# Gate/up of the two feed-forward layers: the last two plain outputs go to other places, and the first combined unit is written in a fixed order on three engines

## The chip, the cores and the metric

One core of one Trainium2 chip runs the whole kernel. The metric is the device time of one execution in microseconds (us). TensorE (PE) does the matrix products, VectorE (DVE), ScalarE (ACT) and GpSimd (POOL) the elementwise work, and SyncE (SP) issues most transfers between memory and the on-chip store.

## The reference

One inference step of a two-layer decoder for a prompt of 1040 rows and 64 sample rows, which share all weights. The part that matters is the feed-forward step behind each layer:

```python
def swiglu(xn, w_gu, w_d):
    gu = xn @ w_gu
    return (jax.nn.silu(gu[..., :D_FF]) * gu[..., D_FF:]) @ w_d
```

`D_MODEL` is 1024 and `D_FF` 2816; the step is done twice, once per layer, as h = h + swiglu(rmsnorm(h)).

## The kernel before

**Tiling.** The 1104 rows lie along the free axis in three groups t = 0, 1, 2 of 336, 384 and 384 columns; a column block of 128 weights is stationary. Every float32 operand is split into a high part (rounded by ACT, `copy` or `Copy` with a scale) and a low part (source minus high part, on DVE), and each product is three matmuls: high by high, low by high, high by low. `self.split(src, hi, lo)` is one such pair of instructions for weights (lines L336 on ACT and L337 on DVE). For activations the pair is `m.cast(r, src)` (L145, or L147 with a sign) on ACT and `m.rest(r, src)` (L141, or L154 with a sign) on DVE.

**Gate and up** (`ffn`). The 22 blocks of 128 gate columns and 22 of up columns are worked as numbered pairs x: even x is gate, odd x is up, each of two blocks (f = 0, 1). Pairs 0 and 1 are "plain": `direct(x, t)` does 48 matmuls for one row group and returns two evictions, `ends`. For gate an eviction is ACT's Silu from the accumulator into a `spare` place. For up it is DVE's product of the accumulator with that place, and a transfer of the product to `hT` (lines L1484 and L1485):

```python
tt(out=o, in0=b, in1=o, op=ALU.mult)
nc.sync.dma_start(hT[t][:, f], o)
```

Pairs 2 to 21 are "combined" units. A `Unit(x)` uses 20 products of sums of weights with sums of activations instead of 24 (a fast matrix-multiplication scheme over 2 blocks x 3 row groups). `u.p(r, b)` is product r, six matmuls into bank b (L1331); `u.copy` moves a bank to a place c on ACT (L1337); `u.mark` adds or subtracts a bank and a place on DVE (L1306 adds, L1307 subtracts); `u.out` is ACT's Silu (L1353) for gate, or DVE's product with the kept gate value (L1350) and a transfer to `hT` for up. The places have names (s1, c15, s2, e, t4, v2); for unit 2 the rotation in `Unit.__init__` makes t4 the buffer `ns[:, 1]` and v2 the buffer `fs`, which are also the two `spare` places of row group 2.

`u.steps(v)` is a generator of four steps with 16 products, and the last four (19, 14, 6, 3) of a unit are done within the first two steps of the next (`v` is the unit before). In order: step 0 is 17, copy s1, 15, copy c15, 18, copy s2, 10. Step 1 is 8, copy e, mark e (which reads the bank of product 10), 9, copy t4, 2, copy v2, mark t4, 13. Product 13 is the first to write that bank anew, so it needs mark e done. Step 2 is 12, mark s1, 5, 16, mark s1, Silu, 1, mark v2, 4, mark v2, Silu. Step 3 is 7, mark t4, 11, mark c15, Silu, 0, mark c15, Silu.

**Weights of a unit.** `weights.load(x)` brings the two blocks of pair x with SP. `weights.sums(x, part)` makes 12 sums on POOL (L108) into staging places. `weights.split(x, g)` splits block g of the products' weights: blocks 0 to 4 are (17, 15, 18, 10), (8, 2, 9, 13), (12, 1, 5, 4), (14, 0, 11, 7) and (6, 3); products that lie side by side are one instruction (15, 18 and 10 are 768 columns wide, 17 alone 256).

**What sets the order.** The program is planned by a scheduler with a model of the engines' times. Under `manual_schedule` the named engines keep the written order. `order` pins PE, DVE and ACT from the last group of the projection before to the end of the plain pairs; then `order.close()`, and `with fixed()` pins PE alone for units 2 to 20. Instructions of ACT and DVE behind `order.close()` are placed where the scheduler's model has the engine free, also in front of pinned ones. Two more casts stand in the unit loop of unit 2: the activations of products 7 and 3 of row group 2 (`m.cast`, `m.rest`), in steps 1 and 2.

Of the kernel before, what the change touches and what calls it, by code (L numbers as in the profile page):

```python
# [11 lines left out]
ALU = mybir.AluOpType  # L12
# [18 lines left out]
SL = max(b - a for a, b in TS)  # L31
# [3 lines left out]
NF = DFF // P  # L35
# [90 lines left out]
class Mix:  # L126
# [7 lines left out]
    def y(self, k, t, n=SL):  # L134
        return self.H[t][:, 2 * k : 2 * k + 2, :n]
# [1144 lines left out]
def ffn(self, H, flat, l, weights, order, mix, small, each, after, end, early=None):  # L1280
# [3 lines left out]
    nc, I = self.nc, self.I  # L1284
# [4 lines left out]
    hT = [self.dram.tile([P, NF, n], F32, name=f"hT{l}_{t}") for t, n in enumerate(size)]  # L1289
    with self.pool(f"ffn{l}") as fp, self.pool(f"ffnp{l}", space=PSUM) as pp:  # L1290
# [7 lines left out]
        col = lambda h, o: flat[h][:, o : o + SL]  # L1298
# [6 lines left out]
        tt = nc.vector.tensor_tensor  # L1305
# [158 lines left out]
        m, y = mix, mix.y  # L1464
# [6 lines left out]
        def direct(x, t):  # L1471

            n, ends = size[t], []
            for f in range(2):
                w = [a.rearrange("p (k n) -> p k n", k=KT) for a in weights.plain(x, f)]
                b = bank("mp", "d")[:, :n]
                for j in range(KT):
                    k = 2 * (ks if t == 2 else (2, 1, 3, 0))[j // 2] + j % 2
                    a = [z[:, k % 2] for z in m.X[m.D[t][k // 2]]]
                    self.mm3(b, w[0][:, k], w[1][:, k], a[0], a[1], j == 0, j == KT - 1)  # L1480

                def evict(b=b, o=spare[t][f][:, :n], f=f):
                    if x:
                        tt(out=o, in0=b, in1=o, op=ALU.mult)  # L1484
                        nc.sync.dma_start(hT[t][:, f], o)  # L1485
                    else:
                        nc.scalar.activation(o, b, AF.Silu)
                ends.append(evict)
            return ends
# [73 lines left out]
        weights.split(2, 2)  # L1563
        ends[1]()
        weights.sums(3, slice(0, 9))
        order.close()
        with fixed():
            v = None
            for x in range(2, NF - 1):
                u = Unit(x)  # L1570
                for g, _ in enumerate(u.steps(v)):
                    if x == 2 and 0 < g < 3:
                        r, src = ((7, y(2, 2)), (3, y(3, 2)))[g - 1]
                        m.cast(r, src, -1.0)
                        m.rest(r, src, -1.0)
                    if g < 3:
                        if g < 1 or g < 2 < x:
                            weights.split(x, 3 + g)
                        weights.split(x + 1, g)
                    if g == 1:  # L1580
                        weights.sums(x + 1, slice(9, None))
                        if x + 2 < NF:
                            weights.load(x + 2)
                    if g == 3 and x + 2 < NF:
                        weights.sums(x + 2, slice(0, 9))
                v = u
        with fixed(E.DVE, E.Activation):
            u = Unit(NF - 1)
# [33 lines left out]
            for i, (t, z, c) in enumerate(seq):  # L1622
# [4 lines left out]
                for m in range(4):  # L1627
                    if lead:
                        acc[m] = bank("dps", "d")
                    o = acc[m][:, :n]  # L1630
# [19 lines left out]
                if i in (2, 16, 38):  # L1650
                    y = (2, 16, 38).index(i)
# [941 lines left out]
```

## Time and profile before

| what | value |
|---|---|
| median of 3 runs | 2955.42 us (2948.49 to 2958.77) |
| the profiled execution | 2959.27 us, span 2957.4 us |
| PE busy | 2836.6 us, 96% of the span |
| DVE, ACT, POOL busy | 1708.2, 1305.3, 999.5 us |
| units 2 to 21, first layer | from 635.9 us |
| units 2 to 21, second layer | from 2244.9 us |

A line of the timeline has the start in us, the length in us, the engine, the line of the kernel, the operation, what it writes and reads, its shape and a count; in brackets stands how long the engine had been idle before and what ended that. In the first layer the weights' raw places carry the name vA, in the second Ht; `slot`, `wl0` and `wl1` are weight places, `x0`, `x1`, `x2`, `T` and `U` activation places, `m` and `mp` accumulators. Matmuls overlap, so the distance of two starts tells more than a length.

### The profile page before, as it was taken

How to read it: one execution, taken by the hardware profiler on the slowest of the kernel's cores; microseconds unless marked ns; L12 is line 12 of the kernel's file. 1: busy time of each engine (PE TensorE's matmuls, PEld its weight loads, DVE VectorE, ACT ScalarE, POOL GpSimd, SP SyncE). 2: the span in 40 equal slices, each digit the busy share in tenths (PEclk: the TensorE clock that was granted, in tenths of full speed). 3: DMA queues.
4: the chain of work that ended last, by engine and by line, in shares of the span. 5: the costliest groups of instructions: out<-in, count | busy, mean ns of one | idle time of the engine just before them, and what ended most of it. 6: DMA issues, size and time to landing. Idle time of an engine off the chain costs nothing.

```text
span 2957.4 us, 53672 instructions
## 1 busy us (share of the span) xinstructions
PE 2836.6 (96%) x20542; PEld 2711.6 (92%) x20542; DVE 1708.2 (58%) x3406; ACT 1305.3 (44%) x2591; POOL 999.5 (34%) x1480
## 2 busy tenths in 40 slices
PE   7999997989999999999999899999998999999999
PEld 7998886989999999999999887777898999999998
DVE  5032456687777855463354442677467787765543
ACT  5122364344444444343344453777444444443432
POOL 2011223145556511104353101454315656541110
PEclk9999898999999999999999999999999999999999
DMA  7052446222222266544354676443412222227652
GB/s 224 7 134 86 117 112 186 82 62 76 79 77 85 84 244 214 172 152 152 125 166 136 200 286 216 152 157 101 143 55 72 80 81 78 78 83 262 211 183 102
DMA packets 300139, 392.79 MB, mean 133 GB/s; under 512 B 32238, under 2 KB 222698, under 8 KB 298858
## 3 DMA queue, kind: packets, MB, share of 16 engines
q1 hardware_dynamic: 262978, 270.05, 28.5%
q0 software_dynamic: 33232, 117.01, 11.9%
q8 instruction: 161, 2.64, 0.4%
q10 hardware_dynamic: 3672, 2.31, 0.3%
q14 instruction: 96, 0.79, 0.1%
HBM read 292.19 MB, written 97.10 MB: 132 GB/s over the span
## 4 chain that ended last, share of the span: by engine, by line
PE 70%; DVE 9%; ACT 4%; issue 4%; DMA 2%; POOL 1%; DVEq 0%; ACTq 0%; POOLq 0%; SPq 0%
PE m L1331 24%; PE dps L266 6%; PE dps L268 6%; PE dps L267 6%; PE tmps L266 3%; PE tmps L267 3%; PE tmps L268 3%; PE pops L268 2%; PE pops L266 2%; PE pops L267 2%; PE sp L2380 1%; DVE slot L337 1%; PE op L2467 1%; DVE s L2384 1%; PE bps L266 1%
## 5 line engine op out<-in xcount | busy, mean ns | idle before, releaser
L337 DVE TENSOR_TENSOR slot<-slot,slot 128x1024 fp32r<-128x1024 f32 (+3 forms) x264 | 270.5, 1027 | 131.8 <-ACT slot L336 125.4
L336 ACT CAST slot<-slot 128x1024 fp32r<-128x1024 f32 (+3 forms) x264 | 208.0, 790 | 249.1 <-PE dps L267 92.4
L1331 PE MATMUL m<-x1h,slot 128*128 128x384 f32 x640 | 176.7, 337 | 0.0
L1331 PE MATMUL m<-x0h,slot 128*128 128x336 f32 x640 | 168.1, 317 | 0.0
L1331 PE MATMUL m<-x2h,slot 128*128 128x384 f32 x480 | 135.5, 337 | 0.0
L409 POOL TENSOR_TENSOR ns<-ns,nq 128x384 f32<-128x384 f32 (+1 forms) x60 | 63.4, 1056 | 198.1 <-ACT nq L407 196.7
L1438 POOL DMA_DIRECT2D hr<-hT x60 | 32.5, 542 | 287.3 <-DVE T_2l L337 69.0
L108 POOL TENSOR_TENSOR slot<-Ht 128x256 f32<-128x256 f32 x80 | 75.8, 959 | 150.4 <-DMA Ht<-in_w_gate_up 146.6
L108 POOL TENSOR_TENSOR slot<-vA 128x256 f32<-128x256 f32 x80 | 74.8, 946 | 152.7 <-DMA vA<-in_w_gate_up 148.2
L337 DVE TENSOR_TENSOR slot<-Ht,slot 128x256 fp32r<-128x256 f32 (+3 forms) x101 | 85.3, 846 | 63.9 <-ACT slot L336 63.9
L337 DVE TENSOR_TENSOR slot<-vA,slot 128x256 fp32r<-128x256 f32 (+3 forms) x101 | 85.4, 847 | 63.4 <-ACT slot L336 63.4
L1331 PEld LDWEIGHTS m<-x1h,slot 128*128 128x128 f32 x640 | 116.8, 188 | 0.1
L1331 PEld LDWEIGHTS m<-x0h,slot 128*128 128x128 f32 x640 | 114.0, 189 | 0.0
L1331 PE MATMUL m<-x1l,slot 128*128 128x384 f32 x320 | 107.5, 336 | 0.0
L1331 PE MATMUL m<-T_2h,slot 128*128 128x384 f32 x320 | 98.3, 348 | 6.9 <-ACT ns L1337 4.4
L1331 PE MATMUL m<-x0l,slot 128*128 128x336 f32 x320 | 101.6, 317 | 0.0
L2407 ACT ACTIVATE s<-s,nb 128x272 f32<-128x272 f32 (+7 forms) x126 | 98.9, 786 | 0.0
L1331 PE MATMUL m<-T_4h,slot 128*128 128x384 f32 x320 | 97.2, 345 | 0.0
L2442 ACT COPY th<-tp 128x768 f32<-128x768 f32 (+1 forms) x80 | 73.4, 919 | 53.8 <-PE tp L2434 30.8
L108 POOL TENSOR_TENSOR Ht<-Ht 128x512 f32<-128x512 f32 (+1 forms) x60 | 85.3, 1422 | 29.3 <-DVE wl1l L337 29.3
L108 POOL TENSOR_TENSOR vA<-vA 128x512 f32<-128x512 f32 (+1 forms) x60 | 85.4, 1424 | 28.4 <-DVE wl0l L337 28.4
L1834 DVE TENSOR_REDUCE ss<-sqb 128x4 f32<-128x256 f32 (+1 forms) x72 | 30.2, 419 | 101.8 <-ACT sqb L1833 101.0
(813 smaller groups left out, 10354.4 us busy)
## 6 DMA issues: line engine op xcount, KB each, us to landing
slot<-in_w_down SPq DMA_DIRECT2D x88, 512.0 KB
wr<-in_w_down SPq DMA_DIRECT2D x42, 512.0 KB
vA<-in_w_gate_up SPq DMA_DIRECT2D x40, 512.0 KB
Ht<-in_w_gate_up SPq DMA_DIRECT2D x40, 512.0 KB
hr<-hT POOLq DMA_DIRECT2D x46, 384.0 KB, 5.1
kp<-in_cache_k SPq DMA_DIRECT2D x32, 512.0 KB
vp<-in_cache_v SPq DMA_DIRECT2D x32, 512.0 KB
wraw<-in_w_in_a SPq DMA_DIRECT2D x24, 512.0 KB
```

The source lines that it names most:

```text
L108: self.net.nc.gpsimd.tensor_tensor(out=o, in0=a, in1=b, op=op)
L266: mm(ps, sh, mh, start=first, stop=False)
L267: mm(ps, sh, ml, start=False, stop=False)
L268: mm(ps, sl, mh, start=False, stop=last)
L336: self.nc.scalar.copy(hi, src)
L337: self.nc.vector.tensor_tensor(out=lo, in0=src, in1=hi.bitcast(F32), op=ALU.subtract)
L409: (nc.vector if x >= late else nc.gpsimd).tensor_tensor(out=s, in0=s, in1=sq, op=ALU.add)
L1331: nc.tensor.matmul(u.b[b][:, :n], w[p][:, k], x[q][:, k], start=new and k == i == 0, stop=k == 1 and i == 2, skip_group_check=True)
L1438: nc.gpsimd.dma_start(hraw[j], hT[t][:, 2 * c : 2 * c + 2])
L1834: nc.vector.tensor_reduce(out=ss[:m, i, :], in_=sq[:m].rearrange("p (h d) -> p h d", d=DH), op=ALU.add, axis=AX.X)
L2407: nc.scalar.activation(ss[z, u], ss[z, u], AF.Exp, bias=nb[:, z : z + 1], accum_out=sm[:, u, z : z + 1])
L2442: nc.scalar.copy(th.rearrange("p x z (u h q) -> p h (x z u) q", h=2, q=64)[:, :, :n], pt[:, :, :n])
```

## The change

The products of pair 1 for row group 2 are written to `nr` and to a free part of the first row group's buffer, and no longer over the Silu values. Unit 2 is taken out of the loop and written out ahead of `order.close()`, so that its ACT and DVE instructions are pinned, its copies, marks and Silus included. The splits of unit 3's blocks 0, 1 and 2 stand one step later than they did: block 0 behind step 1, block 1 behind step 2, block 2 behind step 3. The casts for products 7 and 3 stand behind steps 1 and 2 as before, now in a fixed place beside these splits. The sums for unit 4 keep their step.

```diff
                 def evict(b=b, o=spare[t][f][:, :n], f=f):
                     if x:
-                        tt(out=o, in0=b, in1=o, op=ALU.mult)
-                        nc.sync.dma_start(hT[t][:, f], o)
+                        g = o
+                        if t == 2:
+                            g = (self.nr, col(0, 7 * SL))[f]
+                        tt(out=g, in0=b, in1=o, op=ALU.mult)
+                        nc.sync.dma_start(hT[t][:, f], g)
...
         ends[1]()
         weights.sums(3, slice(0, 9))
+        u = Unit(2)
+        for g, _ in enumerate(u.steps(None)):
+            if g == 0:
+                weights.split(2, 3)
+            if g == 1:
+                m.cast(7, y(2, 2), -1.0)
+                m.rest(7, y(2, 2), -1.0)
+                weights.split(3, 0)
+                weights.sums(3, slice(9, None))
+                weights.load(4)
+            if g == 2:
+                weights.split(3, 1)
+                m.cast(3, y(3, 2), -1.0)
+                m.rest(3, y(3, 2), -1.0)
+            if g == 3:
+                weights.split(3, 2)
+                weights.sums(4, slice(0, 9))
         order.close()
         with fixed():
-            v = None
-            for x in range(2, NF - 1):
+            v = u
+            for x in range(3, NF - 1):
                 u = Unit(x)
                 for g, _ in enumerate(u.steps(v)):
-                    if x == 2 and 0 < g < 3:
-                        r, src = ((7, y(2, 2)), (3, y(3, 2)))[g - 1]
-                        m.cast(r, src, -1.0)
-                        m.rest(r, src, -1.0)
                     if g < 3:
-                        if g < 1 or g < 2 < x:
+                        if g < 2:
                             weights.split(x, 3 + g)
                         weights.split(x + 1, g)
```

## The prediction

> **What bounds the kernel now.** I read the page first, then the waits of PE in the two stretches where unit 2 runs, then the timelines of PE, ACT and DVE there, and last the table of busy times in the stretches behind.
>
> ```profile
> span 2957.4 us, 53672 instructions
> PE 70%; DVE 9%; ACT 4%; issue 4%; DMA 2%; POOL 1%; DVEq 0%; ACTq 0%; POOLq 0%; SPq 0%
> ```
>
> Of the chain that ended last 70% is PE. So a microsecond that PE loses is lost to the kernel, unless a later wait swallows what is won. The waits of PE around unit 2, in the first layer and in the second:
>
> ```profile
> PE m L1331 <- DVE vA L1306: 5.3, 1, 5.3
> PE m L1331 <- ACT ns L1337: 2.0, 1, 2.0
> PE m L1331 <- ACT vA L1337: 1.9, 1, 1.9
> ```
>
> ```profile
> PE m L1331 <- DVE Ht L1306: 5.7, 1, 5.7
> PE m L1331 <- ACT ns L1337: 1.9, 1, 1.9
> ```
>
> Each wait occurs once per layer: two for ACT's copies out of a bank (s1, then e) and one for DVE's mark e (L1306). Together PE stands still 9.2 us in the first layer and 7.6 in the second. The timeline of PE, first layer and then second:
>
> ```profile
> 637.68 0.32 PE L1331 MATMUL m<-x0h,slot 128*128 128x336 f32 x1
> 640.02 0.44 PE L1331 MATMUL m<-T_2h,slot 128*128 128x384 f32 x1 [2.02 <-ACT ns L1337]
> 648.35 0.48 PE L1331 MATMUL m<-x0h,slot 128*128 128x336 f32 x1
> 654.13 0.69 PE L1331 MATMUL m<-U_6h,slot 128*128 128x384 f32 x1 [5.30 <-DVE vA L1306]
> 656.22 0.52 PE L1331 MATMUL m<-T_4h,slot 128*128 128x384 f32 x1
> 661.96 0.34 PE L1331 MATMUL m<-x2h,slot 128*128 128x384 f32 x1
> 664.04 0.32 PE L1331 MATMUL m<-x0h,slot 128*128 128x336 f32 x1
> 665.89 0.35 PE L1331 MATMUL m<-x1h,slot 128*128 128x384 f32 x1
> ```
>
> ```profile
> 2262.44 0.69 PE L1331 MATMUL m<-U_6h,slot 128*128 128x384 f32 x1 [5.69 <-DVE Ht L1306]
> 2273.91 0.35 PE L1331 MATMUL m<-x1h,slot 128*128 128x384 f32 x1
> ```
>
> U_6 is product 13, T_4 here is 12, x2 is 4 and 7, the x0 at 664.04 is 11 and 0, and the x1 at 665.89 opens unit 3. These rows give the price of a product. Products 4 and 7 take 664.04 - 661.96 = 2.08, so 1.04 each; 11 and 0 take 1.85, so 0.93 each. Product 13, right behind the long wait, takes 656.22 - 654.13 = 2.09, twice as much. The table of busy times shows why (the column before the last two is the granted clock):
>
> ```profile
> 654.00:656.00 2.00, 1.87 (x6) 1.87 (x7) 1.45 (x3) 0.00 (x0) 2.00 (x3) 0.50 0.00 0
> 2250.00:2252.00 2.00, 2.00 (x9) 2.00 (x8) 2.00 (x3) 0.48 (x1) 2.00 (x3) 0.56 0.16 40
> ```
>
> After the 5.3 us wait the clock is 0.50. It also falls, to 0.56, in the second layer after the wait of only 1.9 us.
>
> **ACT's part.** The two short waits come from the order on ACT:
>
> ```profile
> 636.54 0.85 ACT L147 ACTIVATE x2h<-vA 128x768 fp32r<-128x768 f32 x1
> 638.76 0.84 ACT L147 ACTIVATE x2h<-vA 128x768 fp32r<-128x768 f32 x1
> 639.51 0.46 ACT L1337 COPY ns<-m 128x384 f32<-128x384 f32 x1
> 650.73 0.44 ACT L1337 COPY fs<-m 128x336 f32<-128x336 f32 x1 [1.68 <-DMA hT<-fs]
> ```
>
> The casts for products 7 and 3, written behind steps 1 and 2, ran before copy s1, though product 17 was done at about 637.1 (15 ends at 637.68 + 0.32 = 638.0 and takes 0.93). Pinned, ACT does copy s1 at 637.1, copy c15 at 638.0 when 15 ends, and copy s2 at 639.0 when 18 ends. PE then goes 17, 15, 18 without a gap: 18 starts at 637.9 and not 640.02. Then ACT does the two casts of split(2, 3) (768 and 256 columns, at 0.85 for 768 some 1.2 us) to about 640.8, ahead of copy e, which is free at 641.05 when 8 ends. Product 9 follows at about 641.6 (a gap of 0.5 left of 1.9), product 2 ends at 643.6.
>
> The last row is what the moved outputs remove: copy v2 goes to `fs`, and waited 1.68 us until the transfer of pair 1's output from `fs` had read it. Pinned, that wait would hold all of ACT behind it. With the product in another place, copy v2 only needs DVE's product to have read `fs`, at about 644.7. I put the two other targets at no cost: same operation and size, one transfer each, issued at the same point. `nr` is next written by unit 3, some 20 us later.
>
> **DVE's part, which decides.** Product 13 waits for mark e:
>
> ```profile
> 636.41 0.97 DVE L337 TENSOR_TENSOR slot<-vA,slot 128x256 fp32r<-128x256 f32 x1
> ...
> 643.11 2.08 DVE L337 TENSOR_TENSOR slot<-vA,slot 128x512 fp32r<-128x512 f32 x2
> 645.11 1.48 DVE L154 SCALAR_TENSOR_TENSOR x2l<-vA,x2h 128x768 fp32r<-128x768 f32 x1
> 646.51 0.54 DVE L1484 TENSOR_TENSOR fs<-mp,fs 128x384 f32<-128x384 f32 x1
> 646.98 1.02 DVE L337 TENSOR_TENSOR slot<-vA,slot 128x768 fp32r<-128x768 f32 x1
> 647.92 2.03 DVE L154 SCALAR_TENSOR_TENSOR x2l<-vA,x2h 128x768 fp32r<-128x768 f32 x1
> 649.87 0.94 DVE L337 TENSOR_TENSOR slot<-vA,slot 128x256 fp32r<-128x256 f32 x1
> 650.73 1.47 DVE L337 TENSOR_TENSOR slot<-slot,slot 128x768 fp32r<-128x768 f32 x1
> 652.13 1.48 DVE L337 TENSOR_TENSOR slot<-vA,slot 128x256 fp32r<-128x256 f32 x1
> 653.53 0.55 DVE L1306 TENSOR_TENSOR vA<-m,vA 128x384 f32<-128x384 f32 x1
> 654.41 1.04 DVE L1306 TENSOR_TENSOR ns<-ns,fs 128x336 f32<-128x336 f32 x1
> ```
>
> ```profile
> 2251.38 1.22 DVE L337 TENSOR_TENSOR slot<-Ht,slot 128x512 fp32r<-128x512 f32 x1
> 2253.93 1.49 DVE L337 TENSOR_TENSOR slot<-Ht,slot 128x768 fp32r<-128x768 f32 x1
> ```
>
> DVE has no gap here: it is late, and five things stand ahead of mark e (653.53) that the pinned order puts behind it. By start to start they are the rest for product 7 (645.11 to 646.51, 1.40), the rest for product 3 (647.92 to 649.87, 1.95), block 0 of unit 3 (17, then 15, 18 and 10: 0.86 and 1.40), and product 8 of unit 3 (1.40): 7.0 us. What stays ahead of mark e: products 5 and 4 of split(2, 2) (1.14, as the second layer's 2251.38 to the rest behind it at 2252.52), the last output (0.47), products 14, 0 and 11 (0.94 here, 1.41 in the second layer) and 7 (0.86). From 643.11 that is 643.11 + 1.14 + 0.47 + 0.94 to 1.41 + 0.86 = 646.5 to 647.0. PE started 0.60 us after mark e (654.13 - 653.53), so product 13 starts at 647.1 to 647.6, before 654.13: 6.5 to 7.0 us earlier. In the second layer 2251.38 + 1.14 + 0.47 + 1.41 + 0.86 + 0.60 = 2255.9, against 2262.44: 6.6 us. So the earlier copies of ACT win nothing by themselves: PE gets to product 13 sooner, and then waits 643.6 to 647.35 for DVE.
>
> Behind mark e the deferred work comes ahead of mark s1, for which product 1 waits: mark e 0.47, mark t4 0.95, the rest for 7 1.40, block 0 of unit 3 2.26, mark s1 0.56, together 5.6 us from the start of mark e: 652.4 in the first layer, 2260.9 in the second. PE meanwhile has 13, 12, 5 and 16: 4 x 1.04 = 4.2 us at full clock, and about 2 x 2.09 + 1.7 = 5.9 if the clock falls as it did. So product 1 starts at 652.5 (DVE the later) to 653.3 (PE the later). Then 1, 4 and 7 (3.12) and 11 and 0 (1.85) follow, and unit 3 opens at 657.5 to 658.3 and not 665.89; in the second layer at 2266.0 to 2266.8 and not 2273.91. Gain 7.6 to 8.4 and 7.1 to 7.9: 14.7 us with the fall of the clock, 16.3 without. I take the fall, because a wait of 1.9 us sufficed for 0.56 in the row above and 3.75 us remain.
>
> The Trainium skill, "TensorE: Matmul & The Clock Gate", section "What's actually happening", has the clock halve only after at least one idle window of about 3.4 us, at a phase that is not tied to the kernel. By that rule a gap of 3.75 us would hardly ever hold a whole window, and the sum would be 16.3. The 0.56 behind a 1.9 us gap does not agree with it, so I stay with the row.
>
> **What is given back in unit 3.** Its product 19 writes a bank that mark c15 of unit 2 reads, and on DVE that mark now stands behind block 1 of unit 3 and the rest for product 3, and this behind ACT's Silus. Counting ACT's pinned order (two Silus at the 0.46 of a copy, four casts of 256, 256, 512 and 768 columns at 0.85 for 768, 2.0 us) I get, as an estimate, mark c15 read at about 660.5 where PE is there at 659.3, and copy s1 of unit 3 behind split(3, 2) up to 0.7 us late. I take 1.2 us per layer of the possible 0 to 1.9: 2.4 us. Total gain 14.7 - 2.4 = 12.3, say 12 us.
>
> **What passes it on.** SP's load for unit 4 needs block 3 of unit 2 split, now at 646.9, before at 645.1 (the end of the two instructions from 643.11). POOL, by its timeline, comes to unit 4's sums later than that:
>
> ```profile
> 653.29 2.76 POOL L108 TENSOR_TENSOR slot<-vA 128x256 f32<-128x256 f32 x3
> ```
>
> So the load stays hidden. The sums, 0.92 each, then wait for unit 3's blocks to be split and end near 665. Unit 4's first block needs three of the first four only, and can't be split before unit 3's product 10 has read the one before it, near 658.3 + 1.2 + 5 x 1.04 + 0.93 = 665.6. Behind gate/up PE is saturated:
>
> ```profile
> 671.94 0.96 DVE L337 TENSOR_TENSOR slot<-vA,slot 128x768 fp32r<-128x768 f32 x1 [4.07 <-ACT slot L336]
> ```
>
> ```profile
> 1070.00:1150.00 80.00, 80.00 (x516) 80.00 (x515) 36.90 (x39) 31.98 (x39) 12.43 (x17) 1.00 0.68 239
> ```
>
> PE is busy for 80.00 of 80 us in the down stage, so no transfer sets the pace there, and I pass the gain on whole. The profiled execution's 2959.27 would become 2947; against the median of the runs, 3.9 us lower, 2943.4.
>
> **Rivals.** *The stall moves to unit 3 (slower).* The pin ends one unit later. DVE and ACT carry the deferred work (unit 3's blocks 0 to 2, both rests) into unit 3, whose own marks are unpinned and can be placed behind it. If unit 3 waited at its product 13 as unit 2 did, with the slow clock behind it, the price would be about what unit 2 lost: the waits of 9.2 and 7.6 plus slow matmuls, 12 to 14 us per layer. It decides from about 7.5 us per layer on, where unit 2's gain is eaten; at full price the result is near 2966. Against it speaks the row at 671.94: DVE stands idle 4.07 us early in unit 3, so it catches up there. *Half the gain is given back (same).* Pinned ACT and DVE wait in turn for each other and for POOL's sums; 3 to 5 us per layer come back in units 2 and 3, partly through the clock: about 2950. *The pin does not do what it says (same).* The trace shows unpinned work in front of pinned (the rest at 645.11 ahead of the output at 646.51), so later work may still be placed ahead of mark e: 2955. Against it: the work that did so is itself pinned now, and what follows needs buffers that unit 2 still uses.
>
> **How the numbers follow.** Forecast 0.60, slower rival 0.17, half given back 0.16, no effect 0.07. A change below 0.3% (8.9 us) can't be told from none. The forecast's own range is a gain of 8 to 17, 2938 to 2947, with a small part short of 8.9; so faster 0.60, same 0.23, slower 0.17. The range reaches up to the half gain and to no effect, 2955, and down to 2934, where DVE's splits would take their shorter forms (0.94 and not 1.41).
>
> **What would show it.** Right: in the changed trace copy s1 starts within 0.3 us of product 17's end; mark e ahead of both L154 rows; product 13's wait at 3 to 4 us and not 5.3 to 5.7; unit 3 opens 20.5 to 24 us after unit 2 (before: 30.0 and 29.0). Wrong: a wait of over 5 us at product 13 or at unit 3's products, or an equal advance at unit 3 that is gone by the down stage.

## The result and the profile after

The kernel with the change takes 2941.66 us (median, 2933.71 to 2952.12), the kernel before in the same comparison 2953.01 (2947.45 to 2963.42). The ratio is 0.996, with a 95% interval of 0.9945 to 0.9976: faster by 0.4%, or 11.35 us between the medians. The forecast was 2943.4. The profiled execution took 2934.39 us, against 2959.27 before, a larger difference; where that comes from is told below.

The head of the page, its busy times and its chain of waits:

```profile
span 2932.7 us, 53641 instructions
...
PE 2820.7 (96%) x20542; PEld 2696.2 (92%) x20542; DVE 1704.8 (58%) x3406; ACT 1305.9 (45%) x2591; POOL 1002.1 (34%) x1480
...
PE 67%; DVE 11%; ACT 4%; issue 4%; DMA 2%; POOL 1%; DVEq 0%; ACTq 0%; POOLq 0%; SPq 0%
```

PE is busy for 96% of the span in both kernels, and the chain of waits is again mostly PE (67%, before 70%). The waits of PE around units 2 and 3, first layer and then second (us in total, times, longest):

```profile
PE m L1331 <- DVE vA L1306: 2.9, 2, 2.0
PE m L1331 <- ACT vA L1337: 1.4, 2, 0.8
```

```profile
PE m L1331 <- DVE Ht L1306: 2.9, 2, 2.1
PE m L1331 <- ACT Ht L1337: 0.9, 3, 0.6
```

One of the three short waits in the last row (0.20 us, at 2283.31) lies in unit 4 already. For the second layer of the kernel before, the view of PE's waits has a row beside the two that the prediction shows:

```profile
PE m L1331 <- ACT Ht L1337: 0.6, 1, 0.6
```

So within units 2 and 3 PE now stands still 4.3 and 3.7 us, where it was 9.2 and 8.2. The timeline of PE in the first layer, and the three rows of the second that answer to it:

```profile
624.50 0.34 PE L1331 MATMUL m<-x1h,slot 128*128 128x384 f32 x1
...
629.56 0.45 PE L1331 MATMUL m<-T_1h,slot 128*128 128x384 f32 x1 [0.81 <-ACT vA L1337]
...
631.46 0.45 PE L1331 MATMUL m<-U_9h,slot 128*128 128x384 f32 x1 [0.57 <-ACT vA L1337]
...
635.75 0.45 PE L1331 MATMUL m<-U_6h,slot 128*128 128x384 f32 x1 [2.04 <-DVE vA L1306]
...
640.59 0.34 PE L1331 MATMUL m<-x1h,slot 128*128 128x384 f32 x1
...
646.60 0.34 PE L1331 MATMUL m<-x1h,slot 128*128 128x384 f32 x1
...
648.66 0.44 PE L1331 MATMUL m<-x1h,slot 128*128 128x384 f32 x1 [0.84 <-DVE vA L1306]
...
668.26 0.34 PE L1331 MATMUL m<-x1h,slot 128*128 128x384 f32 x1
```

```profile
2226.42 0.34 PE L1331 MATMUL m<-x1h,slot 128*128 128x384 f32 x1
...
2237.07 0.44 PE L1331 MATMUL m<-U_6h,slot 128*128 128x384 f32 x1 [2.10 <-DVE Ht L1306]
...
2247.89 0.34 PE L1331 MATMUL m<-x1h,slot 128*128 128x384 f32 x1
```

The rows are: unit 2 opens (624.50), product 8, product 9, product 13, product 16 (640.59), unit 3 opens (646.60), product 19 of unit 2, unit 4 opens (668.26). In the second layer: unit 2 opens, product 13, unit 3 opens. So unit 3 opens 22.10 us after unit 2 in the first layer (30.02 before) and 21.47 in the second (29.00 before). DVE around mark e, the row at 635.16:

```profile
633.34 1.89 DVE L337 TENSOR_TENSOR slot<-vA,slot 128x768 fp32r<-128x768 f32 x2
635.16 0.54 DVE L1306 TENSOR_TENSOR vA<-m,vA 128x384 f32<-128x384 f32 x1
635.63 0.56 DVE L1306 TENSOR_TENSOR ns<-ns,fs 128x336 f32<-128x336 f32 x1
636.11 2.04 DVE L154 SCALAR_TENSOR_TENSOR x2l<-vA,x2h 128x768 fp32r<-128x768 f32 x1
638.07 0.95 DVE L337 TENSOR_TENSOR slot<-vA,slot 128x256 fp32r<-128x256 f32 x1
638.95 1.49 DVE L337 TENSOR_TENSOR slot<-slot,slot 128x768 fp32r<-128x768 f32 x1
640.36 0.55 DVE L1307 TENSOR_TENSOR ns<-m,ns 128x384 f32<-128x384 f32 x1
```

The rest for product 7 (L154) and block 0 of unit 3 now come behind mark e and mark t4, and ahead of mark s1 (640.36). The rest for product 3 and the other splits of unit 3 follow later still. DVE has no gap here, as before: the work is the same, in another order.

Two lengths are used from here on: from the start of unit 2 to the start of unit 3, and to the start of unit 4. The second holds what unit 3 gives back. In the first layer it is 668.26 - 624.50 = 43.76 us after, and 50.50 before.

| kernel | unit 2 to unit 3, 1st / 2nd layer | unit 2 to unit 4 | time, us | ratio to before (95%) |
|---|---|---|---|---|
| before | 30.02 / 29.00 | 50.50 / 49.46 | 2953.01 | 1 |
| after | 22.10 / 21.47 | 43.76 / 43.14 | 2941.66 | 0.996 (0.9945 to 0.9976) |
| e1_outputs_only | 30.23 / 28.63 | 50.71 / 49.09 | 2951.87 | 0.9998 (0.9981 to 1.0015) |
| e2_pin_old_outputs | 23.00 / 22.08 | 44.65 / 43.70 | 2942.22 | 0.9959 (0.9942 to 0.9976) |
| e3_pin_dve_alone | 22.96 / 22.36 | 43.45 / 42.84 | 2935.43 | 0.9931 (0.9906 to 0.9956) |
| e7_rests_ahead | 25.22 / 25.45 | 45.70 / 45.91 | 2952.26 | 0.9991 (0.9974 to 1.0008) |
| a_changed_again | 22.07 / 21.47 | 43.71 / 43.10 | 2938.54 | 0.9963 (0.9946 to 0.9981) |
| e4_pin_act_alone | 21.58 / 21.37 | 42.78 / 42.53 | 2938.57 | one execution |
| e6_splits_later | 20.06 / 19.39 | 45.02 / 44.32 | 2938.96 | one execution |
| e8_rest_behind_s1 | 18.73 / 17.98 | 42.14 / 41.37 | 2934.31 | 0.9947 (0.9928 to 0.9967) |
| e9_unit3_pinned | 18.85 / 18.00 | 43.87 / 42.75 | 2938.08 | 0.9949 (0.9932 to 0.9967) |
| e10_unit3_act_pinned | 18.74 / 18.02 | 42.91 / 42.15 | 2937.21 | one execution |

Each ratio is taken against the runs of the kernel before that belong to the same comparison (their medians lie between 2949.77 and 2953.78 us); it is not the quotient of two times of this table. The lengths come from one profiled execution of each kernel.

The change is worth 50.50 - 43.76 = 6.74 us in the first layer and 49.46 - 43.14 = 6.32 in the second, 13.06 in all, which the interval for the whole time (7.1 to 16.2 us) contains. The two profiled executions differ by 24.7. Of that, 635.87 - 624.50 = 11.4 us lie before unit 2, in code that is the same in both kernels (more on this in the last section), 6.74 in the first layer, 0.4 between the layers and 6.32 in the second.

### The profile page after: what moved, and what is told of

Its sections match the earlier page's. It is cut to its first block, busy times and chain, and to the rows that moved or that the text cites. A ratio compares the mean times of both kernels' runs of the same rounds, so it can differ in the third digit from the quotient of the medians.

```text
span 2932.7 us, 53641 instructions
## 1 busy us (share of the span) xinstructions
PE 2820.7 (96%) x20542; PEld 2696.2 (92%) x20542; DVE 1704.8 (58%) x3406; ACT 1305.9 (45%) x2591; POOL 1002.1 (34%) x1480
## 4 chain that ended last, share of the span: by engine, by line
PE 67%; DVE 11%; ACT 4%; issue 4%; DMA 2%; POOL 1%; DVEq 0%; ACTq 0%; POOLq 0%; SPq 0%
PE m L1331 23%; PE dps L266 6%; PE dps L267 6%; PE dps L268 6%; PE tmps L266 3%; PE tmps L267 3%; PE tmps L268 3%; PE sp L2396 1%; DVE slot L337 1%; PE pops L268 1%; PE op L2483 1%; PE pops L266 1%; PE pops L267 1%; DVE s L2400 1%; PE bps L266 1%
```

## The experiments

Each one changes either which order is pinned or where a step stands. The theory throughout was that the gain is DVE's order ahead of mark e. The rivals give it to ACT's earlier copies, to the moved outputs, or to a wait that another place sets.

**Outputs alone (e1_outputs_only).** The kernel before with only the first piece of the diff, the moved outputs; unit 2 stays unpinned.

```diff
-                        tt(out=o, in0=b, in1=o, op=ALU.mult)
-                        nc.sync.dma_start(hT[t][:, f], o)
+                        g = o
+                        if t == 2:
+                            g = (self.nr, col(0, 7 * SL))[f]
+                        tt(out=g, in0=b, in1=o, op=ALU.mult)
+                        nc.sync.dma_start(hT[t][:, f], g)
```

> The kernel before with only the two last outputs of pair 1 written elsewhere; unit 2 stays unpinned and no instruction changes its place. Measure: first matmul of unit 2 to first matmul of unit 3, first and second layer (before 30.0 and 29.0 us, after 22.1 and 21.5). Theory (DVE's order ahead of mark e sets the stage): copy v2 no longer waits 1.68 us for the transfer, but mark t4 stands behind mark e anyway, so 30.0 and 29.0 within 0.3, product 13 still waits over 5 us, ratio 1.000. Rival (the outputs' place is the gain): 1.7 us shorter per layer, 28.3 and 27.3.

PE's wait for mark e, first and second layer:

```profile
PE m L1331 <- DVE vA L1306: 5.7, 1, 5.7
```

```profile
PE m L1331 <- DVE Ht L1306: 5.6, 1, 5.6
```

It is as long as before, and the two layers together are as long as before (50.71 + 49.09 = 99.80 against 99.96). By themselves the new places bring nothing. In the second layer 28.63 lies 0.07 outside what the theory allowed; the first, 30.23, is as long as before.

**The order alone (e2_pin_old_outputs).** The changed kernel with that first piece of the diff undone.

```diff
-                        tt(out=g, in0=b, in1=o, op=ALU.mult)
-                        nc.sync.dma_start(hT[t][:, f], g)
+                        tt(out=o, in0=b, in1=o, op=ALU.mult)
+                        nc.sync.dma_start(hT[t][:, f], o)
```

> The changed kernel with the last outputs of pair 1 in their old places; unit 2 pinned, every engine's order as in the changed kernel. Theory: product 13 starts as early as in the changed kernel, but copy v2 waits for the transfer from fs (3.7 us from the product to the copy in the trace of before), and pinned ACT and DVE wait behind it by about 2 us, so product 1 is 1.3 to 1.6 us later: 23.4 to 23.8 and 22.8 to 23.2 us. Rival (the outputs' place does not matter): 22.1 and 21.5.

One row each of ACT, DVE and PE:

```profile
650.97 0.44 ACT L1337 COPY fs<-m 128x336 f32<-128x336 f32 x1 [3.49 <-DMA hT<-fs]
```

```profile
651.44 0.87 DVE L1306 TENSOR_TENSOR ns<-ns,fs 128x336 f32<-128x336 f32 x1 [1.56 <-ACT fs L1337]
```

```profile
656.54 0.45 PE L1331 MATMUL m<-x1h,slot 128*128 128x384 f32 x1 [2.12 <-DVE ns L1307]
```

Here the chain can be read row by row: copy v2 waits 3.49 us for the transfer out of `fs`, mark t4 on DVE waits 1.56 for copy v2, and with it all that stands behind it down to mark s1, for which product 1 waits 2.12 us. It costs 0.89 and 0.56 us up to unit 4, less than expected. In the first layer part of the wait takes the place of the clock's fall, as products 13 and 12 run at full speed here (1.16 and 1.06 us); in the second layer the clock falls to 0.50 (2254 to 2256 us), product 12 takes 1.9 us, and product 1 waits only 0.46. So with the pin the new places are worth something, but they carry only about a tenth of its 6.3 to 6.7 us, and in the whole time the two kernels can't be told apart.

**DVE's order without ACT's (e3_pin_dve_alone).** Unit 2 stands in a block of its own that pins PE and DVE; ACT is left to the scheduler.

```diff
+        order.close()
+        with fixed(E.DVE):
-        u = Unit(2)
-        for g, _ in enumerate(u.steps(None)):
+            u = Unit(2)
+            for g, _ in enumerate(u.steps(None)):
...
-        order.close()
```

> The changed kernel with PE and DVE pinned in unit 2 but ACT left to the scheduler: ACT gets its old order (casts for products 7 and 3 ahead of copy s1), DVE keeps mark e ahead of the deferred work. Theory: the two short waits of PE for ACT's copies come back (2 us each) and are covered by the wait for mark e; copy v2 comes about 1 us later, so 22.3 to 23.5 and 21.7 to 22.9 us. Rival (the gain is ACT's earlier copies): it loses the two short waits again, about 4 us per layer, 25.5 to 26.5 us.

The waits of PE in the first layer:

```profile
PE m L1331 <- ACT ns L1337: 2.0, 1, 2.0
PE m L1331 <- DVE ns L1307: 1.7, 1, 1.7
```

Apart from these two, PE waits only 0.24 us in unit 2, at product 9. The old wait for copy s1 is back in full (2.0 us), and the gain stays: 22.96 and 22.36 to unit 3, and to unit 4 even 0.3 us less than the change. The rival that gives the gain to ACT's early copies falls. DVE's order decides, and PE's 2 us on the way to product 13 are 2 us that it does not wait there.

**Both rests ahead of mark e again (e7_rests_ahead).** ACT's copies stay early; only the two casts and rests move.

```diff
             if g == 0:
                 weights.split(2, 3)
-            if g == 1:
                 m.cast(7, y(2, 2), -1.0)
                 m.rest(7, y(2, 2), -1.0)
+                m.cast(3, y(3, 2), -1.0)
+                m.rest(3, y(3, 2), -1.0)
+            if g == 1:
...
-                m.cast(3, y(3, 2), -1.0)
-                m.rest(3, y(3, 2), -1.0)
```

> The changed kernel with the casts and rests for products 7 and 3 written behind step 0, so that 3.4 to 3.9 us of DVE's work go back in front of mark e; ACT still does the copies s1, c15 and s2 early. Theory: product 13 starts 3.4 to 3.9 us later, its wait grows from 2.0 to over 5 us and the clock falls behind it; 25.0 to 26.5 us in the first layer and 24.4 to 26.0 in the second. Rival A (ACT's copies are the gain): 22 us as in the changed kernel. Rival B (only DVE's total up to mark s1 counts, since product 1 waits for it): 22 to 23 us.

DVE ahead of mark e (653.71) in the first layer:

```profile
648.54 1.89 DVE L337 TENSOR_TENSOR slot<-vA,slot 128x768 fp32r<-128x768 f32 x2
650.35 3.43 DVE L154 SCALAR_TENSOR_TENSOR x2l<-vA,x2h 128x768 fp32r<-128x768 f32 x2
653.71 0.54 DVE L1306 TENSOR_TENSOR vA<-m,vA 128x384 f32<-128x384 f32 x1
```

The two rests are one row of 3.43 us, start to start 3.36, and product 13 starts 3.4 and 3.2 us later than after the change. That is the price of two instructions on DVE, one to one. The waits at product 13 are 2.7 and 4.5 us, less than expected: the casts, which move too, hold up copy e on ACT, and PE gets there later itself. Of the gain 1.9 and 2.8 us less reach unit 4. In the whole time the kernel can't be told from the one before (0.9991), although its two stages are still 8.4 us shorter together, which would be 0.997; that lies just outside the interval, and why is open.

**ACT's order without DVE's (e4_pin_act_alone).** The same block as in e3 with the other engine.

```diff
-        with fixed(E.DVE):
+        with fixed(E.Activation):
```

> The changed kernel with PE and ACT pinned in unit 2 but DVE left to the scheduler. DVE's splits and rests need ACT's casts first, and planned behind a pinned ACT they fall behind mark e by themselves: DVE's order differs from the changed kernel's by one exchange behind mark s1. Theory (the length follows DVE's order, however it comes about): 22.1 and 21.5 within 0.3 us. Rival (DVE must be pinned to hold the order): over 25 us.

PE around product 13 in the first layer (13, and 16 at 642.35), and the table of busy times beside it:

```profile
639.07 0.45 PE L1331 MATMUL m<-U_6h,slot 128*128 128x384 f32 x1 [2.04 <-DVE vA L1306]
...
642.35 0.34 PE L1331 MATMUL m<-x1h,slot 128*128 128x384 f32 x1
```

```profile
640.00:642.00 2.00, 2.00 (x13) 2.00 (x12) 2.00 (x2) 0.00 (x0) 2.00 (x2) 1.00 0.79 231
```

The rival expected DVE's old order to return; it did not. With ACT pinned the scheduler put DVE's instructions in the changed order but for one exchange, as I read it because each split and rest on DVE needs ACT's cast first. The 0.5 us by which the first layer is shorter than expected is the clock: behind the same wait of 2.04 us it stayed at 1.00.

**The change once more (a_changed_again).** No edit; it shares the comparison with e4, e6 and e8.

> The changed kernel as it is, beside the others on the same chip. First matmul of unit 2 to first matmul of unit 3 as before: 22.1 and 21.5 us; unit 2 to unit 4: 43.8 and 43.1. Ratio to the kernel before 0.9956, the 13.1 us that the two stages gave.

The lengths repeat within 0.05 us, the ratio within 0.0003.

**Less work ahead of mark e and mark s1 (e6_splits_later, e8_rest_behind_s1).** In e6 the splits of unit 2's block 3 and of unit 3's blocks 0 and 1, and the cast and rest for product 3, stand a step later each. e8 adds to this that the cast and rest for product 7 stand behind mark s1, through a hook in `steps`.

```diff
+        u.mid = lambda: (m.cast(7, y(2, 2), -1.0), m.rest(7, y(2, 2), -1.0))
         for g, _ in enumerate(u.steps(None)):
-            if g == 0:
-                weights.split(2, 3)
             if g == 1:
-                m.cast(7, y(2, 2), -1.0)
-                m.rest(7, y(2, 2), -1.0)
-                weights.split(3, 0)
+                weights.split(2, 3)
...
             if g == 2:
+                weights.split(3, 0)
+            if g == 3:
                 weights.split(3, 1)
```

(e6 keeps the cast and rest for product 7 at `g == 1` and has no hook.)

> The changed kernel with less of DVE's work ahead of mark e and mark s1: split(2, 3) written behind step 1 and not 0, split(3, 0) behind step 2, split(3, 1) and the cast and rest for product 3 behind step 3. Theory: product 13 loses its 2.0 us wait and the fall of the clock behind it, and product 1 then waits 1 to 2 us for mark s1, behind which still stand split(2, 3) and the rest for product 7: 19.8 to 20.6 us in the first layer, 19.2 to 20.0 in the second. Rival (ACT's copies or the clock set the stage): 21 to 22 us.

> The kernel of the run before with the cast and rest for product 7 also moved, behind the first mark s1 of unit 2 (product 7 needs them only three products later). Theory: product 1 no longer waits, PE keeps only the waits for copies s2 and e (0.2 to 0.8 and 0.6 us): 18.3 to 19.0 us in the first layer and 17.7 to 18.4 in the second; unit 2 to unit 4 39.4 to 40.5 and 38.8 to 39.9, so 6 to 8 us less than the changed kernel in all, ratio to the kernel before 0.993. Rival (the work put off is paid back in unit 3): unit 2 to unit 4 within 1 us of the changed kernel's 43.8 and 43.1.

In unit 2 both do what was expected: unit 3 opens at 20.06 and 19.39 us in e6, at 18.73 and 17.98 in e8. But not all of it reaches unit 4. One row each of PE, ACT and DVE of e8, in unit 3, first layer:

```profile
658.81 0.44 PE L1331 MATMUL m<-T_4h,slot 128*128 128x384 f32 x1 [1.82 <-ACT nr L1337]
```

```profile
657.87 0.52 ACT L1353 ACTIVATE vA<-vA 128x384 f32<-128x384 f32 x1 [1.76 <-DVE vA L1307]
658.30 0.46 ACT L1337 COPY nr<-m 128x384 f32<-128x384 f32 x1
```

```profile
655.18 1.30 DVE L337 TENSOR_TENSOR wl0l<-vA,wl0h 128x256 fp32r<-128x256 f32 x1
656.41 0.95 DVE L337 TENSOR_TENSOR slot<-vA,slot 128x256 fp32r<-128x256 f32 x1
657.29 0.55 DVE L1307 TENSOR_TENSOR vA<-m,vA 128x384 f32<-128x384 f32 x1
```

Read from the end: product 12 of unit 3 waits 1.82 us for copy t4 on ACT, that copy stands behind a Silu, the Silu waits 1.76 us for a mark on DVE, and the mark stands behind two splits. So e8 gains 8.4 us of 50.50 in the first layer and 8.1 of 49.46 in the second, where 9.6 to 11.1 had been expected. e6 gains 5.5 and 5.1, less than the change, but not because more work was put off, as e8 puts off more. Its unit 3 lasts 1.5 us longer than e8's in both layers (24.96 against 23.41 in the first) with the same wait of 1.82 us at product 12; behind that wait the clock is 0.50 in e6 (662 to 664 us) and 1.00 in e8 (660 to 662 us). e8 is the best kernel in the stage: 3.4 us shorter than the change in both layers together. In the whole time, 0.9947 against 0.9963 on the same chip, the intervals overlap.

**Unit 3 pinned as well (e9_unit3_pinned, e10_unit3_act_pinned).** I took e8's wait in unit 3 to come from the end of the pin, behind which splits can overtake marks. e9 is e8 with the same pin for unit 3, e10 with ACT alone.

```diff
-        with fixed():
-            v = u
-            for x in range(3, NF - 1):
+        v = u
+        for x in range(3, NF - 1):
+            with fixed(*((E.DVE, E.Activation) if x == 3 else ())):
```

> The kernel with the rest for product 7 behind mark s1, and now ACT and DVE also keep the written order in unit 3. In the run before, unit 3 of that kernel waited 0.30 us at product 10 and 1.8 us at product 12 (for copy t4 on ACT, which stood behind a Silu whose mark e on DVE stood behind two splits of later weights, 2.2 us). Theory (where the pin ends, unpinned splits get ahead of the next unit's marks, the small form of what the change removed from unit 2): the 1.8 us wait goes, unit 2 to unit 4 falls from 42.1 and 41.4 to 40.0 to 40.8 and 39.3 to 40.1 us, and no equal wait appears in unit 4; ratio to the kernel before 0.993. Rival (the wait at product 12 is work put off from unit 2, on engines that are full): 41.5 us and more, or the wait shows up again at a neighbouring product.

> As the run beside it, but in unit 3 only ACT keeps the written order and DVE is left to the scheduler. Theory, from the run with ACT pinned alone in unit 2: DVE's order follows ACT's, so within 0.5 us of the run beside it (40.0 to 40.8 and 39.3 to 40.1). Rival (DVE's marks are overtaken again): the 1.8 us wait at product 12 stays, 42.1 and 41.4.

DVE in unit 3 of e9, first layer, and PE's product 13 there:

```profile
665.88 4.41 DVE L337 TENSOR_TENSOR slot<-vA,slot 128x512 fp32r<-128x512 f32 x4
670.21 2.06 DVE L337 TENSOR_TENSOR slot<-slot,slot 128x768 fp32r<-128x768 f32 x1
672.19 0.55 DVE L1306 TENSOR_TENSOR vA<-m,vA 128x384 f32<-128x384 f32 x1
```

```profile
672.79 0.44 PE L1331 MATMUL m<-U_6h,slot 128*128 128x384 f32 x1 [1.51 <-DVE vA L1306]
```

That theory fell. The wait of 1.82 us at product 12 becomes one of 1.51 us at product 13 of unit 3 (1.52 in the second layer), for mark e behind five split instructions, with 0.54 left at product 12, and both kernels reach unit 4 later than e8: by 1.7 and 1.4 us with both engines, by 0.8 and 0.8 with ACT alone. Not all of e9's 1.7 us is waiting: in the first layer PE waits 2.23 us in unit 3, against 2.12 in e8, and the clock falls to 0.50 (676 to 678 us), where it stayed at 1.00 in e8; in the second layer it stays at 1.00, and PE waits 3.2 us, 0.99 of them for DVE at product 1. So the written order moves what is given back, and does not remove it. I read it as put-off work that DVE still has to do within units 2 and 3; this is not shown by a run of its own. How the splits would have to be spread over more units was not tried.

## Why the prediction was right, and where a size was off

**DVE's sum ahead of mark e held.** It put product 13 at 11.2 to 11.7 us after the opening of unit 2 in the first layer and 11.0 in the second. Measured are 635.75 - 624.50 = 11.25 and 2237.07 - 2226.42 = 10.65, against 18.26 and 17.53 before. e7 confirms its largest term: two rests put back cost 3.4 and 3.2 us where the sum has 3.35. And with mark e ahead of both rests (L154) the rival by which the pin does not hold falls.

**The wait at product 13 was mis-sized:** 3 to 4 us forecast, 2.04 and 2.10 measured. DVE is on time; in the first layer PE comes 1.5 us later than I had it (633.71, that is 9.2 us after the opening, not 7.7). In the second it comes 0.8 us later (8.55), and product 13 starts 0.3 earlier than forecast. The step that failed is copy s2 "at 639.0 when 18 ends". Two rows of ACT:

```profile
625.74 0.48 ACT L1337 COPY ns<-m 128x384 f32<-128x384 f32 x1 [0.78 <-PE m L1331]
...
629.03 0.48 ACT L1337 COPY vA<-m 128x384 f32<-128x384 f32 x1 [1.92 <-DVE x1l L141]
```

Copy s1 does start with product 17's end, as forecast: its idle time was ended by PE, whose last matmul of 17 ends at 625.71. But copy s2 writes the place that the rest for product 19 (L141) still reads on DVE, and waits 1.92 us for it, so product 8 waits 0.81, the largest part of the 1.5. I had followed each copy to its bank and not to the place it writes. It cost nothing, since DVE sets when product 13 starts.

**The fall of the clock behind that wait came,** though the wait was only 2 us. That was luck as much as forecast: in the first layer of e2 and of e4 the clock stayed up behind the same wait. DVE's sum up to mark s1 held beside it, at 5.75 us where the forecast had 5.6, but also because two of its terms were off by about as much in opposite directions: mark t4 took 0.48 us start to start and not 0.95, the rest for product 7 took 1.96 and not 1.40. Product 1 starts about 17.1 us after the opening (forecast 16.6 to 17.4), and unit 3 opens at 22.10 and 21.47 (forecast 21.6 to 22.4 and 21.1 to 21.9).

**What unit 3 gives back** was 1.2 us per layer in the forecast. Unit 3 lasts 43.76 - 22.10 = 21.66 and 21.67 us, against 20.48 and 20.46 before: 1.18 and 1.21. It is at the named place:

```profile
645.11 1.19 DVE L337 TENSOR_TENSOR slot<-slot,slot 128x256 fp32r<-128x256 f32 x2
646.35 1.37 DVE L154 SCALAR_TENSOR_TENSOR x2l<-vA,x2h 128x768 fp32r<-128x768 f32 x1
647.64 0.55 DVE L1307 TENSOR_TENSOR ns<-m,ns 128x384 f32<-128x384 f32 x1
648.11 0.49 DVE L1306 TENSOR_TENSOR vA<-m,vA 128x336 f32<-128x336 f32 x1
```

Mark c15 (648.11) stands behind block 1 of unit 3 and the rest for product 3, and product 19 starts behind it at 648.66, after 0.84 us. The slower rival, the stall that moves to unit 3, is in the trace in this small form only. The copy s1 of unit 3, up to 0.7 us late in the forecast, ends no wait of PE there; the 1.2 us, chosen between 0 and 1.9, came out this well partly by chance. The rival with 3 to 5 us per layer given back asked for more than twice as much.

**The gain is passed on whole.** From the opening of unit 4 in the second layer to the end of the span it is 663.0 us before and 663.1 after. The sum of both layers is 13.06 us, where the forecast had 14.7 - 2.4 = 12.3. That the median of 2941.66 lies only 1.7 us from the forecast is in part chance: the forecast started from a median of 2955.42 over three runs, and over fourteen runs it is 2953.01.

**A reading that was wrong.** The prediction has PE stand still 7.6 us in the second layer before; it left out the row of 0.6 us shown above, and it is 8.2. Only the price of the slower rival used this figure; the gain was summed from starts.

## What to carry to other kernels

Where an engine without a gap feeds the one that bounds the kernel, count the instructions that stand ahead of the one being waited for, start to start: this sum was right to half a microsecond, and the gaps of every other engine before that point were worth nothing. Work that is put off is not gone; look for the next instruction behind which it then stands, and set what the next unit pays against what this one wins (in the first layer e8 wins 3.4 us more than the change in unit 2 and pays 1.8 more in unit 3). Before two variants are ranked by such a stage, read the granted clock behind their waits: it alone was 1.5 us between e6 and e8. Of a copy that is moved ahead, follow both its ends: the bank it reads and the last reader of the place it writes.

## What was unexpected of the hardware

**The clock behind a short wait.** After the change the three products 13, 12 and 5 take 640.59 - 635.75 = 4.84 us, and the table of busy times shows the clock:

```profile
638.00:640.00 2.00, 2.00 (x8) 2.00 (x7) 2.00 (x3) 0.00 (x0) 2.00 (x3) 0.50 0.20 60
```

In e4 the same three products behind the same wait take 642.35 - 639.07 = 3.28 us, at 1.00. Whether 2 us of waiting cost 1.6 us more is thus not set by the wait alone; e6 and e8 show the same behind a wait of 1.82 us. What sets it was not tried. The Trainium skill, "TensorE: Matmul & The Clock Gate", section "What's actually happening", has the clock judged in windows whose phase is not tied to the kernel, and these pairs fit that. The whole idle window of about 3.4 us that the Trainium skill asks for there does not fit: gaps of 2.04 and 1.82 us were enough here.

**Most of the spread comes from a far stage.** The opening of unit 2 in the first layer lies between 624.5 and 640.5 us in the profiles of these kernels, though the code ahead of it is the same in all. It goes with the clock granted between 240 and 360 us, here of after, before and e9, in which unit 2 opens at 624.50, 635.87 and 640.5:

```profile
240.00:360.00 120.00, 109.82 (x712) 97.56 (x711) 44.65 (x125) 33.81 (x75) 27.30 (x43) 0.94 0.41 111
```

```profile
240.00:360.00 120.00, 109.95 (x663) 97.40 (x662) 39.64 (x112) 30.16 (x67) 25.56 (x40) 0.89 0.41 109
```

```profile
240.00:360.00 120.00, 110.49 (x619) 97.29 (x619) 38.19 (x109) 25.33 (x50) 24.28 (x38) 0.83 0.37 99
```

The other profiles fall in line: at 0.93 or 0.94 unit 2 opens between 624.5 and 630.4 us, at 0.89 at 633.6 and 635.9, at 0.83 between 638.6 and 640.5. Between two executions the spread is up to 16 us, more than the change itself; paired by the same instructions of ACT, the trace of e9 falls behind that of after by about 11 of them between 240 and 360 us. So a difference of two profiled executions says little here, and the lengths of the stage itself were compared instead. What makes the clock differ in that stage was not tried.
